# Layer seams of a fused two-block kernel: weights split ahead, and where the low part of the inputs is computed

## The chip, the cores and the metric

The kernel runs on one core of a Trainium2 chip. The metric is the time of one launch on the device in microseconds (us); the median over several runs counts. TensorE (PE) multiplies, VectorE (DVE), ScalarE (ACT) and GpSimd (POOL) do elementwise work, SyncE (SP) issues the loads. Each engine runs its own queue in order and waits for semaphores of the others.

## The reference, cut to what matters

Two blocks follow each other on a 512 x 1024 stream `x`, of two layers each. The first has an attention and convolution layer (called layer 0) and a gated recurrent one (layer 1), each closed by a scaled residual and a layer norm. The second block has an even mixer, an FFN, an odd mixer and an FFN:

```python
def rms_norm(x, g):
    y = x32 * rsqrt(mean(x32 * x32, axis=-1) + NORM_EPS) * g

def swiglu(x, w_gate, w_up, w_down):
    return (silu(x @ w_gate) * (x @ w_up)) @ w_down

for layer in range(DEPTH):
    hn = rms_norm(x, norm_mix_pre[layer])
    mix = even_mixer(hn, ...) if layer % 2 == 0 else odd_mixer(hn, ...)
    x = x + rms_norm(mix, norm_mix_post[layer])
    hn = rms_norm(x, norm_ffn_pre[layer])
    ff = swiglu(hn, w_gate[layer], w_up[layer], w_down[layer])
    x = x + rms_norm(ff, norm_ffn_post[layer])
```

The odd mixer is a projection, a convolution over four positions, two gates (matrix products), a linear recurrence and a product with a second, activated projection. Everything is float32.

## The kernel before

`x` lies transposed in SBUF: eight tiles `res_x` of 128 features x 512 positions. A matrix with float32 accuracy is multiplied in three passes: each operand is split into a rounded high part and a rest, and `product` (L303) runs high x high, high x low and low x high for each of the eight 128-blocks of the inner dimension, 24 matmuls for one output block.

`weights` (L244 and L250 through the helpers) loads a block of 128x1024 into `wp_r`, ACT copies it to the rounded `wp_h`, and DVE, or POOL where it is asked for, subtracts: `wp_l = wp_r - wp_h`. The pool has three `wp_r` and four of `wp_h` and `wp_l` each, so at most four split blocks are ahead.

The end of a layer is `out_products`: the first five output blocks over all columns, then the last three (`keep`) in two halves of 256 columns. `use` takes each result off PSUM (tiles `po_mx` in the mixers, `g_ff` in the FFN) and adds its square to `po_a`. `done(s)` then sums `po_a` over the features with a matmul against ones (the tile `z`), gets the reciprocal root (ACT, then the three DVE operations on `po_t` and `po_r`) and walks over the eight `m` of that half: a product with `po_r`, an update of `res_x`, and `pre(m, s)`. In layers 0 and 1 `deepnorm` has the same part with mean and variance (`n_a`, `n_m`, `n_r`).

`pre` (L1054) makes the next layer's inputs. ACT writes `pn_h = res_x * scale` (with a bias as well at the end of layer 1), ACT copies it to the rounded `act_h`, and POOL subtracts: `act_l = pn_h - act_h`. These are 16 tiles of 128x256 at each of four places: from layer 1 to the even mixer, from there to its FFN, from this FFN to the odd mixer, and from there to its FFN.

The next layer begins with `firsts`: three weight blocks, whose subtractions run on POOL, and the first three products, one half of the columns after the other, `k` by `k`, so that PE can start on a half as soon as its first `act_h` and `act_l` are there. The pre-norm's own scale (`res_acc`, summed by `rms` into the tile `g` or `z`) comes later and is multiplied onto the results, so the products don't wait for it. In the odd mixer `rms` stands right behind `firsts`; then come the convolution (`o_xb`, `o_xc`), whose split result `o_h` and `o_l` feeds the gates, products into `g`.

No order is written out by hand: a scheduler places each engine's instructions by priorities that follow the order of the program, and a tile of a pool is taken again when its last reader is done.

Of the kernel before, what the change touches and what calls it, by code (L numbers as in the profile page):

```python
# [188 lines left out]
class Prog:  # L189
    def __init__(self, es, tc, I, off):  # L190
        self.tc, self.nc, self.I, self.off, self.es = tc, tc.nc, I, off, es
        nc = self.nc
# [146 lines left out]
    def out_products(self, ps, block, xs, parts, use, done, keep=3, n=1024, late=(), begun=None, spare=(None, 0)):  # L339
# [108 lines left out]
    def layer0(self, stop=False):  # L448

        nc, tc = self.nc, self.tc  # L450
        with ExitStack() as es:
# [78 lines left out]
            self.out_products(ps, lambda m: self.I["wo_ab"][m], xs2, PARTS, use, done, spare=(Alloc(es, tc, "w0", {"h": (1, 1024), "l": (1, 1024)}), 1))  # L530
# [282 lines left out]
    def layer1(self):  # L813
        nc, tc = self.nc, self.tc
        with ExitStack() as es:
# [24 lines left out]
            self.out_products(ps, lambda m: self.I["wo_c"][m], xs2, PARTS[:2], use, done, spare=(Alloc(es, tc, "w5", {"h": (1, 1024), "l": (1, 1024)}), 1))  # L840
# [570 lines left out]
    def even(self):  # L1411
        tc = self.tc
        with ExitStack() as es:
# [6 lines left out]
            self.out_products(ps, lambda m: self.I["wo_ev"][m], xs2, PARTS[:2], use, done, late=(4, 5), begun=begun, spare=(Alloc(es, tc, "w6", {"h": (2, 1024), "l": (2, 1024)}), 2))  # L1420
# [213 lines left out]
    def odd(self):  # L1634
        tc = self.tc
        with ExitStack() as es:
# [235 lines left out]
```

## Time and profile before

| | |
|---|---|
| runs | 2127.01, 2133.92, 2132.29 us; median 2132.29 us |
| profiled execution | 2134.38 us, its span 2132.6 us |
| busy share of the span | PE 96%, DVE 63%, ACT 43%, POOL 20% |
| POOL on `act_l` | 64 operations, 56.6 us |
| POOL on `wp_l` | 27 operations, 69.4 us |

The shares are averages over a long program. In the middle of the layers PE is busy without a gap. The transitions are short stretches: layer 0 to layer 1 at 440 to 476 us, layer 1 to the even mixer at 898 to 968, even mixer to its FFN at 1173 to 1222, this FFN to the odd mixer at 1545 to 1612, odd mixer to its FFN at 1735 to 1784. A row's time in square brackets is how long the engine stood idle just before, and what released it. A row that ends in x4 is four instructions that ran on without a gap.

### The profile page before, as it was taken

To read this page: it belongs to the slowest core of one execution; us is meant where nothing else is said; L and a number is where in the kernel's file an instruction comes from. 1 tells how busy PE (TensorE), PEld (TensorE's weight loads), DVE (VectorE), ACT (ScalarE), POOL (GpSimd) and SP (SyncE) were. 2 spreads that over 40 slices of the span, in tenths; PEclk is the share of its full clock that TensorE was granted. 3 is DMA by queue.
4 is the path that set the end of the run, shared out by engine and by line. 5 is a ranking of instruction groups with operands and counts; after the bars stand their busy time and mean duration, and the time that the engine had idled before them with its cause. 6 is when DMAs were issued, how large, how long until landed. Compare 5 with 4: busy or idle time off the path is not lost.

```text
span 2132.6 us, 29872 instructions
## 1 busy us (share of the span) xinstructions
PE 2045.8 (96%) x11624; PEld 1740.2 (82%) x11624; DVE 1349.8 (63%) x2290; ACT 911.0 (43%) x1634; POOL 427.0 (20%) x403
## 2 busy tenths in 40 slices
PE   6999999999999999989999999999989799999997
PEld 4888888889888888888778888888877588888886
DVE  6775566786666665786665734535589886254455
ACT  2563343445433444455655533222356645322231
POOL 1111111354122221042112310101143322010011
PEclk9999999999999999999989999999999899999998
DMA  8344442321111111224423133333312232333231
GB/s 300 119 158 136 146 142 71 116 88 60 50 54 56 50 50 50 89 85 158 119 70 99 60 96 102 99 98 93 116 50 69 70 99 80 109 96 93 98 109 40
DMA packets 80142, 204.97 MB, mean 96 GB/s; under 512 B 19200, under 2 KB 28160, under 8 KB 80000
## 3 DMA queue, kind: packets, MB, share of 16 engines
q1 hardware_dynamic: 80000, 203.06, 30.1%
q8 instruction: 91, 1.49, 0.3%
q14 instruction: 51, 0.42, 0.1%
HBM read 188.87 MB, written 14.16 MB: 95 GB/s over the span
## 4 chain that ended last, share of the span: by engine, by line
PE 76%; DVE 13%; issue 5%; ACT 4%; POOL 1%; DMA 1%; SPq 0%; POOLq 0%; DVEq 0%; ACTq 0%
PE mm L313 56%; PE a L313 5%; PE mc L313 3%; PE x L313 2%; PE S L313 2%; DVE res_x L266 1%; PE s L313 1%; PE pt L651 1%; PE o L313 1%; DVE wp_l L250 1%; PE mc L425 1%; DVE o_xc L266 1%; DVE n_a L250 1%; ACT wp_h L244 1%; PE z L313 1%
## 5 line engine op out<-in xcount | busy, mean ns | idle before, releaser
L244 ACT ACTIVATE wp_h<-wp_r 128x1024 fp32r<-128x1024 f32 (+2 forms) x263 | 271.3, 1037 | 456.1 <-PE mm L313 263.4
L250 DVE TENSOR_TENSOR wp_l<-wp_r,wp_h 128x1024 fp32r<-128x1024 f32 (+1 forms) x236 | 326.9, 1388 | 108.7 <-ACT wp_h L244 108.6
L313 PE MATMUL mm<-act_h,wp_l 128*128 128x512 f32 (+1 forms) x1008 | 379.4, 376 | 12.0 <-DVE wp_l L250 10.2
L313 PE MATMUL mm<-act_l,wp_h 128*128 128x512 f32 (+1 forms) x1008 | 380.0, 377 | 1.9 <-POOL act_l L250 1.9
L313 PE MATMUL mm<-act_h,wp_h 128*128 128x512 f32 (+1 forms) x1008 | 379.8, 377 | 1.7 <-ACT wp_h L244 1.3
L313 PE MATMUL mm<-a_h,wp_h 128*128 128x512 f32 (+1 forms) x920 | 336.8, 367 | 5.5 <-ACT wp_h L244 3.3
L313 PE MATMUL mm<-a_h,wp_l 128*128 128x512 f32 (+1 forms) x920 | 329.8, 359 | 1.2 <-POOL wp_l L250 1.2
L313 PE MATMUL mm<-a_l,wp_h 128*128 128x512 f32 (+1 forms) x920 | 328.6, 358 | 0.9 <-DVE a_l L250 0.9
L313 PEld LDWEIGHTS mm<-act_h,wp_l 128*128 128x128 f32 x1008 | 194.0, 192 | 46.4 <-DVE wp_l L250 11.1
L313 PEld LDWEIGHTS mm<-act_l,wp_h 128*128 128x128 f32 x1008 | 193.6, 192 | 35.9 <-POOL act_l L250 2.6
L313 PEld LDWEIGHTS mm<-act_h,wp_h 128*128 128x128 f32 x1008 | 193.5, 192 | 34.7 <-ACT wp_h L244 1.8
L313 PEld LDWEIGHTS mm<-a_h,wp_h 128*128 128x128 f32 x920 | 174.1, 189 | 30.6 <-ACT wp_h L244 3.3
L313 PEld LDWEIGHTS mm<-a_l,wp_h 128*128 128x128 f32 x920 | 174.1, 189 | 25.9 <-issue 1.9
L313 PEld LDWEIGHTS mm<-a_h,wp_l 128*128 128x128 f32 x920 | 173.8, 189 | 24.6 <-POOL wp_l L250 1.4
L250 POOL TENSOR_TENSOR g_g<-g_g,g_u 128x512 f32<-128x512 f32 x44 | 61.1, 1390 | 549.3 <-DVE g_u L250 502.9
L313 PE MATMUL mm<-h_l,wp_h 128*128 128x512 f32 (+1 forms) x344 | 129.2, 376 | 0.6 <-DVE h_l L250 0.5
L313 PE MATMUL mm<-h_h,wp_h 128*128 128x512 f32 (+1 forms) x344 | 129.0, 375 | 0.3 <-ACT h_h L244 0.3
L313 PE MATMUL mm<-h_h,wp_l 128*128 128x512 f32 (+1 forms) x344 | 128.8, 374 | 0.0
L250 DVE TENSOR_TENSOR g_u<-mm,res_rr 128x512 f32<-128x512 f32 x44 | 30.4, 690 | 125.9 <-PE mm L313 125.9
L250 POOL TENSOR_TENSOR wp_l<-wp_r,wp_h 128x1024 fp32r<-128x1024 f32 x27 | 69.4, 2574 | 135.9 <-ACT wp_h L244 119.0
L244 ACT ACTIVATE m_km<-m_k 128x512 f32<-128x512 f32 x56 | 37.5, 672 | 122.9 <-DVE m_k L250 101.4
L247 ACT ACT_TABLE_LOAD x60 | 77.0, 1283 | 1.8 <-PEq L1860 0.7
(496 smaller groups left out, 3927.3 us busy)
## 6 DMA issues: line engine op xcount, KB each, us to landing
wp_r<-w_gu SPq DMA_DIRECT2D x88, 512.0 KB, 3.5
wp_r<-w_c SPq DMA_DIRECT2D x40, 512.0 KB, 3.5
wp_r<-wada SPq DMA_DIRECT2D x32, 512.0 KB, 3.7
wp_r<-w_d SPq DMA_DIRECT2D x32, 512.0 KB, 3.6
wp_r<-w_ab SPq DMA_DIRECT2D x26, 512.0 KB, 4.8
st_r<-wada SPq DMA_DIRECT2D x16, 512.0 KB, 7.9
wp_r<-w_od SPq DMA_DIRECT2D x16, 512.0 KB, 3.5
s_d<-s_s SPq DMA_DIRECT2D x24, 256.0 KB, 2.4
```

The source lines that it names most:

```text
L244: self.nc.scalar.activation(out=out, in_=in_, func=ACT.Copy, scale=scale)
L247: self.nc.scalar.activation(out=out, in_=in_, func=func, **kw)
L250: (eng or self.nc.vector).tensor_tensor(out=out, in0=a, in1=b, op=op)
L266: self.nc.vector.scalar_tensor_tensor(out=out, in0=a, scalar=s, in1=b, op0=op0, op1=op1)
L313: self.nc.tensor.matmul(out=out, lhsT=a, rhs=b, start=start, stop=stop)
L425: self.nc.tensor.matmul(out=p[32 * k:32 * k + 32, :], lhsT=self.sc[:, 4 * j + k, :], rhs=raw[j][:, k * 256:(k + 1) * 256], start=j == 0, s ...
L651: nc.tensor.transpose(pt[:, i * 128:(i + 1) * 128], P[h][:, i * 128:(i + 1) * 128], self.idn)
```

## The change

Two things change. First, `out_products` gets a list `after`, the next layer's first weight blocks; as many as buffers are free for (two after layers 0 and 1, three at the other places) are loaded and split, on DVE, ahead of the last products, and `firsts` takes them over and makes only the missing ones on POOL. Second, in `pre` without a bias ACT writes the rounded `act_h` directly from `res_x`, and one DVE operation gives `act_l = res_x * scale - act_h`; with a bias the three steps remain, with the subtraction on DVE. In the odd mixer the fourth product, `proj(3)`, is moved ahead of `rms`.

```diff
     def firsts(self, ps, blocks, xs, tags=("mm",) * 3):
-        ws = [self.weights(b, eng=self.nc.gpsimd) for b in blocks]
+        ws = self.ahead + [self.weights(b, eng=self.nc.gpsimd) for b in blocks[len(self.ahead):]]
+        self.ahead = []
...
-    def out_products(self, ..., begun=None, spare=(None, 0)):
+    def out_products(self, ..., begun=None, spare=(None, 0), after=()):
...
         ws = [self.weights(block(8 - keep + j), n, pool=pool if j < own else None) for j in range(keep)]
+        self.ahead = [self.weights(b) for b in after[:4 - keep + own]]
...
         def pre(k, s, x=None, scale=g, bias=None):
-            hi, lo = self.xs[k]
-            h = N("h")
+            hi, lo = (t[:, s] for t in self.xs[k])
             x = self.x[k][:, s] if x is None else x
             if bias is None:
-                self.act(h, x, ACT.Copy, scale=scale[:, k:k + 1])
+                self.act(hi, x, ACT.Copy, scale=scale[:, k:k + 1])
+                self.stt(lo, x, scale[:, k:k + 1], hi.bitcast(F32), ALU.mult, ALU.subtract)
             else:
+                h = N("h")
                 self.act(h, x, ACT.Identity, scale=scale[:, k:k + 1], bias=bias[:, k:k + 1])
-            self.copy(hi[:, s], h)
-            self.sub(lo[:, s], h, hi[:, s].bitcast(F32), nc.gpsimd)
+                self.copy(hi, h)
+                self.sub(lo, h, hi.bitcast(F32))
...
         first = dict(enumerate(self.firsts(ps, [self.I["w_od"][m] for m in range(3)], xs)))
+        first[3] = proj(3), None
         self.rms(ps("g"))
```

The five calls of `out_products` pass `after`: blocks of `w_c` after layer 0, `w_ev` (4, 8, 0) after layer 1, `w_gu0`, `w_od` and `w_gu1` after the others. The last FFN passes none.

On DVE, at the end of the first FFN, from the root of the first half (`po_r`) on, before (`g_ff` is the FFN's output, `mm` PSUM, `vecs` the scales):

```order
L250 TENSOR_TENSOR g_ff<-g_ff,mm 128x256
L250 TENSOR_TENSOR g_ff<-g_ff,po_r 128x256 x2
L250 TENSOR_TENSOR po_a<-po_a,po_sq 128x256
L266 SCALAR_TENSOR_TENSOR res_x<-g_ff,vecs,res_x 128x256 x2
L250 TENSOR_TENSOR g_ff<-g_ff,po_r 128x256 x2
L266 SCALAR_TENSOR_TENSOR res_x<-g_ff,vecs,res_x 128x256
L250 TENSOR_TENSOR g_ff<-g_ff,mm 128x256
L266 SCALAR_TENSOR_TENSOR res_x<-g_ff,vecs,res_x 128x256
L250 TENSOR_TENSOR g_ff<-g_ff,po_r 128x256
L250 TENSOR_TENSOR po_a<-po_a,po_sq 128x256
```

and now, from the same place on:

```order
L251 TENSOR_TENSOR g_ff<-g_ff,mm 128x256
L251 TENSOR_TENSOR g_ff<-g_ff,po_r 128x256 x2
L251 TENSOR_TENSOR po_a<-po_a,po_sq 128x256
L267 SCALAR_TENSOR_TENSOR res_x<-g_ff,vecs,res_x 128x256 x2
L251 TENSOR_TENSOR g_ff<-g_ff,po_r 128x256
L267 SCALAR_TENSOR_TENSOR act_l<-res_x,vecs,act_h 128x256 x2
L267 SCALAR_TENSOR_TENSOR res_x<-g_ff,vecs,res_x 128x256
L251 TENSOR_TENSOR g_ff<-g_ff,mm 128x256
L251 TENSOR_TENSOR g_ff<-g_ff,po_r 128x256
L267 SCALAR_TENSOR_TENSOR act_l<-res_x,vecs,act_h 128x256
L251 TENSOR_TENSOR po_a<-po_a,po_sq 128x256
L267 SCALAR_TENSOR_TENSOR res_x<-g_ff,vecs,res_x 128x256
```

The `act_l` operations have come into DVE's queue, between the updates and ahead of the additions to `po_a`; three of them stand ahead of this second `po_a`, and three more ahead of the last one.

On POOL, from the end of the even mixer to the start of the odd one, before (`g_g` is the FFN's gate product):

```order
L250 TENSOR_TENSOR wp_l<-wp_r,wp_h 128x1024 x3
L250 TENSOR_TENSOR act_l<-pn_h,act_h 128x256 x16
L250 TENSOR_TENSOR g_g<-g_g,g_u 128x512 x22
L250 TENSOR_TENSOR wp_l<-wp_r,wp_h 128x1024 x3
L250 TENSOR_TENSOR act_l<-pn_h,act_h 128x256 x4
L250 TENSOR_TENSOR wp_l<-wp_r,wp_h 128x1024
L250 TENSOR_TENSOR act_l<-pn_h,act_h 128x256 x9
L1675 MEMSET o_xb 128x3 x2
L250 TENSOR_TENSOR act_l<-pn_h,act_h 128x256 x3
L250 TENSOR_TENSOR wp_l<-wp_r,wp_h 128x1024 x2
```

and now:

```order
L251 TENSOR_TENSOR y_y<-y_y,e_vT 128x512 x4
L251 TENSOR_TENSOR g_g<-g_g,g_u 128x512 x22
L251 TENSOR_TENSOR wp_l<-wp_r,wp_h 128x1024
L1680 MEMSET o_xb 128x3 x2
L251 TENSOR_TENSOR wp_l<-wp_r,wp_h 128x1024 x2
```

What is left on POOL at these two transitions is the odd mixer's own weight subtractions and the FFN's products.

On PE, around `rms` of the odd mixer, before (the numbers tell the tiles apart: `mm_14664` is the fourth projection, `mm_14471` the third; `g_14616` is the sum of `rms`):

```order
L313 MATMUL mm_14471<-act_h_13928,wp_l_14466 128x256
L313 MATMUL mm_14664<-act_h_13914,wp_h_14660 128x512
L313 MATMUL mm_14664<-act_l_13915,wp_h_14660 128x512
L313 MATMUL mm_14664<-act_h_13914,wp_l_14661 128x512
L313 MATMUL mm_14664<-act_h_13916,wp_h_14660 128x512
L313 MATMUL g_14616<-res_acc_13931,ones1024_73 128x512
L313 MATMUL mm_14664<-act_l_13917,wp_h_14660 128x512
```

and now (`mm_14558` is the fourth projection, `mm_14683` the fifth):

```order
L315 MATMUL mm_14558<-act_h_13894,wp_l_14555 128x512
L315 MATMUL mm_14558<-act_h_13896,wp_h_14554 128x512
L315 MATMUL mm_14558<-act_l_13897,wp_h_14554 128x512
L315 MATMUL mm_14558<-act_h_13896,wp_l_14555 128x512
L315 MATMUL g_14583<-res_acc_13899,ones1024_73 128x512
L315 MATMUL mm_14683<-act_h_13882,wp_h_14679 128x512
```

Four of the 24 matmuls of the fourth projection stood ahead of the sum, and 45 of the fourth, fifth and sixth between it and the first gate; now all 24 stand ahead of it, and 16 of the fifth between it and the gates.

## Rows read from the trace of the kernel before

**Rows 1.** Windows view: us, busy us (instructions) of PE, PEld, DVE, ACT, POOL, clock, DMA.

```profile
898.00:968.00 70.00, 63.87 (x393) 58.60 (x392) 61.24 (x102) 37.04 (x69) 25.55 (x23) 0.95 0.31 98
1545.00:1612.00 67.00, 56.89 (x331) 49.71 (x330) 57.90 (x89) 36.65 (x69) 24.39 (x26) 0.92 0.15 48
```

**Rows 2.** PE's waits in 898:968, 1173:1222, 1545:1612, 1735:1784: total us, times, longest.

```profile
PE o L313 <- DVE res_x L266: 2.9, 1, 2.9
PE z L313 <- DVE n_a L250: 1.4, 1, 1.4
...
PE z L313 <- DVE po_a L250: 1.8, 1, 1.8
...
PE z L313 <- DVE po_a L250: 4.1, 1, 4.1
PE g L313 <- DVE res_acc L250: 3.9, 1, 3.9
PE g L313 <- DVE o_l L250: 1.7, 1, 1.7
...
PE z L313 <- DVE po_a L250: 2.7, 1, 2.7
```

**Rows 3.** Windows view of PE, odd mixer's end: us, busy (matmuls), granted clock, DMA.

```profile
1754.90:1758.30 3.40, 3.40 (x19) 0.50 0.00 0
1760.30:1763.70 3.40, 3.40 (x31) 1.00 0.00 0
```

**Rows 4.** Timeline of DVE, 1740 to 1772: start, length, line, out<-in, repeats.

```profile
1745.13 0.87 DVE L266 SCALAR_TENSOR_TENSOR res_x<-po_mx,vecs,res_x 128x256 f32<-128x256 f32 x2
1745.92 0.75 DVE L250 TENSOR_TENSOR po_mx<-po_mx,po_r 128x256 f32<-128x256 f32 x2
...
1748.77 0.96 DVE L250 TENSOR_TENSOR po_a<-po_a,po_sq 128x256 f32<-128x256 f32 x1
...
1751.92 0.81 DVE L266 SCALAR_TENSOR_TENSOR res_x<-po_mx,vecs,res_x 128x256 f32<-128x256 f32 x1
...
1753.00 0.94 DVE L250 TENSOR_TENSOR po_a<-po_a,po_sq 128x256 f32<-128x256 f32 x1
...
1755.87 0.42 DVE L266 SCALAR_TENSOR_TENSOR po_t<-z,po_r 128x256 f32<-128x256 f32 x1 [1.00 <-ACT po_r L247]
...
1761.33 1.84 DVE L266 SCALAR_TENSOR_TENSOR res_x<-po_mx,vecs,res_x 128x256 f32<-128x256 f32 x2
```

**Rows 5.** Timeline of POOL, the same stretch.

```profile
1746.94 3.39 POOL L250 TENSOR_TENSOR act_l<-pn_h,act_h 128x256 fp32r<-128x256 f32 x4 [12.98 <-ACT act_h L244]
...
1767.68 1.44 POOL L250 TENSOR_TENSOR act_l<-pn_h,act_h 128x256 fp32r<-128x256 f32 x2 [1.27 <-ACT act_h L244]
```

**Rows 6.** Timeline of DVE, 1545 to 1600.

```profile
1558.65 2.45 DVE L266 SCALAR_TENSOR_TENSOR res_x<-g_ff,vecs,res_x 128x256 f32<-128x256 f32 x1
...
1591.38 6.20 DVE L266 SCALAR_TENSOR_TENSOR o_xc<-o_xb,vecs,o_xc 128x512 f32<-128x512 f32 x6
```

**Rows 7.** Timeline of POOL, the same stretch.

```profile
1558.11 2.71 POOL L250 TENSOR_TENSOR wp_l<-wp_r,wp_h 128x1024 fp32r<-128x1024 f32 x1 [1.91 <-ACT wp_h L244]
```

**Rows 8.** Timeline of DVE, 905 to 960.

```profile
912.84 1.21 DVE L250 TENSOR_TENSOR wp_l<-wp_r,wp_h 128x1024 fp32r<-128x1024 f32 x1
...
931.82 3.45 DVE L250 TENSOR_TENSOR res_x<-res_x,n_r 128x256 f32<-128x256 f32 x2
...
938.46 0.96 DVE L250 TENSOR_TENSOR n_a<-n_a,n_sq 128x256 f32<-128x256 f32 x1
```

**Rows 9.** Timeline of PE, 1576 to 1602.

```profile
1584.25 2.08 PE L313 MATMUL g<-res_acc,ones 128*128 128x512 f32 x2 [3.90 <-DVE res_acc L250]
...
1597.63 1.21 PE L313 MATMUL g<-o_h,wp_h 128*128 128x512 f32 x4 [0.37 <-ACT o_h L244]
```

**Rows 10.** Timeline of POOL, 905 to 960.

```profile
955.95 1.45 POOL L250 TENSOR_TENSOR act_l<-pn_h,act_h 128x256 fp32r<-128x256 f32 x2
```

**Rows 11.** Timeline of ACT, 1740 to 1762.

```profile
1746.46 0.71 ACT L244 ACTIVATE act_h<-pn_h 128x256 fp32r<-128x256 f32 x2
```

More of the change, by code (lines that the diff above doesn't have):

```diff
@@ L299, in firsts @@
     def firsts(self, ps, blocks, xs, tags=("mm",) * 3):
-        ws = [self.weights(b, eng=self.nc.gpsimd) for b in blocks]
+        ws = self.ahead + [self.weights(b, eng=self.nc.gpsimd) for b in blocks[len(self.ahead):]]
+        self.ahead = []
         out = [ps(t) for t in tags]
@@ L337, in scores, with out_products @@
             self.matmul(out, q[h], k[:, cols], i == 0, i == 1)
-    def out_products(self, ps, block, xs, parts, use, done, keep=3, n=1024, late=(), begun=None, spare=(None, 0)):
+    def out_products(self, ps, block, xs, parts, use, done, keep=3, n=1024, late=(), begun=None, spare=(None, 0), after=()):
         wide = [X] + [s for s in parts if s.start >= L]
@@ L529, in layer0 @@
             use, done = self.deepnorm(N, ps, res, mod, emit)
-            self.out_products(ps, lambda m: self.I["wo_ab"][m], xs2, PARTS, use, done, spare=(Alloc(es, tc, "w0", {"h": (1, 1024), "l": (1, 1024)}), 1))
+            self.out_products(ps, lambda m: self.I["wo_ab"][m], xs2, PARTS, use, done, spare=(Alloc(es, tc, "w0", {"h": (1, 1024), "l": (1, 1024)}), 1), after=[self.I["w_c"][m] for m in range(3)])
     def layer0_mix(self, es, e0, late, xs, Y, first, s5):
@@ L839, in layer1 @@
             use, done = self.deepnorm(N, ps, self.x, self.mods[1], emit)
-            self.out_products(ps, lambda m: self.I["wo_c"][m], xs2, PARTS[:2], use, done, spare=(Alloc(es, tc, "w5", {"h": (1, 1024), "l": (1, 1024)}), 1))
+            self.out_products(ps, lambda m: self.I["wo_c"][m], xs2, PARTS[:2], use, done, spare=(Alloc(es, tc, "w5", {"h": (1, 1024), "l": (1, 1024)}), 1), after=[self.I["w_ev"][m] for m in (4, 8, 0)])
             for k in range(KT):
@@ L1419, in even @@
             use, done = self.postnorm(es, ps, "norm_mix_post", 0, pre)
-            self.out_products(ps, lambda m: self.I["wo_ev"][m], xs2, PARTS[:2], use, done, late=(4, 5), begun=begun, spare=(Alloc(es, tc, "w6", {"h": (2, 1024), "l": (2, 1024)}), 2))
+            self.out_products(ps, lambda m: self.I["wo_ev"][m], xs2, PARTS[:2], use, done, late=(4, 5), begun=begun, spare=(Alloc(es, tc, "w6", {"h": (2, 1024), "l": (2, 1024)}), 2), after=[self.I["w_gu0"][m] for m in range(3)])
             stats()
@@ L1642, in odd @@
             use, done = self.postnorm(es, ps, "norm_mix_post", 1, pre)
-            self.out_products(ps, lambda m: self.I["wo_od"][m], xs2, PARTS[:2], use, done, late=(2, 4), spare=(Alloc(es, tc, "w7", {"h": (3, 1024), "l": (3, 1024)}), 3))
+            self.out_products(ps, lambda m: self.I["wo_od"][m], xs2, PARTS[:2], use, done, late=(2, 4), spare=(Alloc(es, tc, "w7", {"h": (3, 1024), "l": (3, 1024)}), 3), after=[self.I["w_gu1"][m] for m in range(3)])
             stats()
@@ L1805, in ffn @@
                     use, done = self.postnorm(es, ps, "norm_ffn_post", l, pre, ff, last)
-                    self.out_products(ps, block, hs, PARTS[:2], use, done, n=n, keep=4 if last else 3, spare=(H, 2))
+                    self.out_products(ps, block, hs, PARTS[:2], use, done, n=n, keep=4 if last else 3, spare=(H, 2), after=() if last else [self.I["w_od"][m] for m in range(3)])
                     if stats:
```

## The prediction

> **What bounds the kernel now.** I read the windows view first, of the places that the change touches. They are the five where one layer ends and the next begins, called seams here: S1 layer 0 to layer 1, S2 layer 1 to even mixer, S3 even mixer to its FFN, S4 that FFN to odd mixer, S5 odd mixer to its FFN. In S2 PE works 63.9 of 70 us and VectorE (DVE) 61.2, in S4 56.9 and 57.9 of 67, GpSimd (POOL) about 25 in each [rows 1]. In the middle of the layers PE has few gaps that this change touches, so these must give what there is. PE's waits say what comes last in them: in S3, S4 and S5 the sum `z` waits for DVE's `po_a` (1.8, 4.1 and 2.7 us), in S4 the rms sum `g` waits 3.9 for DVE's `res_acc` and the gates 1.7 for `o_l`, and in S2 the waits are 2.9 and 1.4 [rows 2].
>
> A wait costs more than its length. The 3.4 us behind S5's wait have a granted clock of 0.50, which is 1.2 GHz, and 19 matmuls; 3.4 us at 1.00 (2.4 GHz) hold 31 [rows 3]. That is 1.3 us lost; I take 1.5 for each such piece, since some records may be missing, and 0.12 us for a matmul of 256 columns, twice that for 512.
>
> The third view is the timeline of DVE against that of POOL. In S5 two products of 128x256 on DVE take 0.75 and two updates of `res_x` 0.87; while POOL's four `act_l` run (1746.94 to 1750.33), an addition `po_a` among them takes 0.96, and two updates at 1761.33 take 1.84 [rows 4, 5]. In S4 one update takes 2.45 while a POOL `wp_l` runs [rows 6, 7]. So a DVE operation that reads two SBUF tensors appears to stand still until POOL's operation is over. This is the lever: what leaves POOL makes other DVE work shorter, while DVE must do the subtraction itself.
>
> The Trainium skill ("SBUF — State Buffer", section SBUF: two separate sides) says that GpSimd and a VectorE operation with two SBUF inputs exclude each other for a whole instruction; the rows agree. Another page of the Trainium skill speaks against the change: "Perfetto Trace Analysis", section Optimizing Scalar/DVE Operations, would offload a saturated DVE to ScalarE or even GpSimd, though it adds that the shared read port may undo the latter. By that rule the seams get slower, which is R3's case below.
>
> **The parts.** Counted on the built kernel: POOL loses 64 `act_l` and 13 `wp_l`, DVE gains these 77, ACT loses 48 scaled copies, PE's work is the same.
>
> Prices. Two updates start 0.79 before the operation behind them [rows 4], so one three-operand operation costs 0.40, and one product likewise 0.34. An `act_l` on DVE has no row; its nearest is the update, the same kind and shape: 0.40 free, 0.92 if slowed as at 1761.33 [rows 4]. I take 0.40, since with POOL's work gone nothing seen in the rows would slow it. Per seam that is 16 x 0.40 = 6.4 us more on DVE.
>
> *S5, worked in full.* Before, the last `po_a` ends at 1753.94 [rows 4] and the last `act_l` at 1767.68 + 1.44 = 1769.1 [rows 5]. In the new order six `act_l` stand ahead of the last `po_a` (+2.4). Against them: three slowed operations (one shown) return from 0.96 to 0.42 (-1.6), the last `po_a` itself from 0.94 (-0.5), an update from 0.81 to 0.40 (-0.4) [rows 4], and two products and an update now stand behind it (-1.1). Sum -1.2. PE has 30 matmuls of the next layer ahead of `z` where it had 19: 11 x 0.12 = 1.3 us of fill. 2.7 - 1.2 - 1.3 leaves a wait of 0.2, and with the wait the slow-clock piece (1.5) should go. What is late next is the second half of the columns. There DVE has a product, an update and an `act_l` per 128 rows, 1.14 us, against nine matmuls or 1.06 on PE, so DVE paces it. From the end of `po_a` (1752.7) to `po_t` it was 1.9 at the slow clock [rows 4], and I take 1.6; two `act_l` in between the three operations up to `po_r` make 2.1, and the rest is 8 x 1.14 plus one `res_acc` addition, 9.7. The last `act_l` ends at 1766.1, that is 3.0 earlier. Gain 3.0, between 1.2 (`po_a` alone) and 4.2 (wait and clock).
>
> *S3* is the same pattern. The wait is 1.8, `po_a` comes 0.8 earlier and 7 matmuls more of fill give 0.8, so it closes. But a `wp_l` (1.2 [rows 8]) that stood ahead of `po_a` now stands behind it, on the way to `po_t`, so the second half gains less: about 2.2. Gain 2.2, between 0.8 and 3.3.
>
> *S4.* `po_a` comes 2.5 earlier (three slowed operations, the 2.45 of [rows 6], two updates moved behind, less 2.4 for `act_l`), the fill is 12 matmuls more (1.4): 4.1 goes to 0.2. By the S5 reckoning the last `act_l` ends 4.5 earlier, the sum of squares `res_acc`, now hit by at most one POOL `wp_l`, gains 1.5 more, and `g` starts near 1578.2 instead of 1584.25 [rows 9], 6.0 earlier. PE doesn't wait there any more, since all 24 matmuls of the fourth product now stand ahead of `g` where 4 stood. But these are taken from the cover behind it: from `g` to the first gate product lie 13.4 us [rows 9], the way through `res_rr`, `o_xb`, the convolution `o_xc` (six updates in 6.2 [rows 6]) and `o_h`. Before, 45 matmuls filled this; now 16 do (3.8 us), and PE waits about 9 us for `o_h`, with a slow-clock piece behind (1.5). At the first gate PE has done 9 of these matmuls less than before (40 instead of 49; 9 x 0.24 = 2.2). So 6.0 - 2.2 - 1.5, and 1.7 back, as the next `o_l` now follows directly on DVE: 4.0. Behind it the mixer waits for DVE and ACT chains which then start 6.0 earlier; between 4.0 and 6.0 I take 4.5. Bounds: 0 (all given back at the gates) and 10 (all waits of S4).
>
> *S2.* Two of three POOL `wp_l` and all `act_l` leave. DVE's two products at 931.82 take 3.45 where two such take 0.75 (-2.7); the order up to the second `z`, relayed at free prices with its eight `act_l`, ends 3.2 before 939.4 [rows 8]. In the second half POOL alternates between `act_l` and scalings of `res_x`; relayed, it gains some 3 more, and the last `act_l`, which ended at 957.4 [rows 10], ends near 951. Two `wp_l` (2.4) come onto DVE ahead of the first `z`, where PE waited 1.4 already. The two waits of [rows 2] and two slow-clock pieces are 7.3 together, and more than that can't come back. I take 5, between 2 and 7.3.
>
> *S1 and the weights ahead.* In S1 two of the three first weights go to DVE early, but the third stays on POOL at its old place, and it is this one that PE's product waits for. Gain 0, between -1 and +1. Elsewhere the early split counts only as POOL time removed, which is in the sums above. The loads of these weights go through the same queue in nearly the same order: 0.
>
> The steady parts of FFNs and mixers are unchanged: 0. **Sum:** 3.0 + 2.2 + 4.5 + 5 = 14.7. The profiled execution took 2134.38 us (span 2132.6); it becomes 2119.7. The median of the runs is 2132.29, 2.1 lower: 2117.6, so 2118.
>
> **Rivals.**
> R1, *the waits only move.* `act_l` stands in DVE's queue and needs ACT's `act_h`, two of which take 0.71 [rows 11]; an update must end first, then ACT, then the handover, while DVE waits with all that is queued behind. At 0.3 for each of four to nine places per seam this is 1.2 to 2.7, in S2, S3 and S5 about 7 together, and S4 returns its 4.5 at the gates: 14.7 - 7 - 4.5 = 3.2 us, time 2129. For it: DVE is near full [rows 1]. Against it: the new order puts a product or an update between in most places.
>
> R2, *everything goes.* All these waits and the clock pieces vanish: 7.3 + 3.3 + 10 + 4.2 = 25, time 2107. For it: every one of the waits in S2, S3 and S5 hangs on a DVE operation that POOL slowed. Against it: the chain behind `g` in S4, and DVE's pace of 1.14 against 1.06.
>
> R3, *slower: DVE becomes the bound.* If DVE's long operations have another cause than POOL (traffic of ACT or PE, say), they stay long and the 16 `act_l` come on top. If half of these cost 0.92 and half 0.40, the second half's share is 5.3, less about 1.2 for the shorter way through ACT and POOL: 4 us later in each of S3, S4 and S5, nothing gained in S2: 2132 + 12 = 2144. It decides from the point at which a three-operand 128x256 operation there stays above 0.6. Against it: the long ones [rows 4, 6] lie inside POOL operations, and those outside are short.
>
> R4, *the change doesn't do what it says:* the weights were already split in time, so splitting ahead is worth nothing. My sum has that in it; only if `act_l` on POOL weren't the lever either, this gives 2132, and it shares R1's chance.
>
> **How the numbers follow.** Forecast, 2112 to 2124: 0.60. R1 with R4: 0.18. R2: 0.13. R3: 0.09. A measurement of this kernel can tell about 0.3% from no change, 6.4 us. The forecast and R2 lie wholly below 2125.9 (0.73), and with a sliver of R1: faster 0.74; same 0.18; slower 0.08. The range runs from 2106 (just below R2) to 2131 (R1 and half of R4), which leaves out R3 and a little of R4 and R2.
>
> **What would show it.** Right: in the changed trace no 128x256 DVE operation in S3 and S5 above 0.5; `act_l` near 0.40; the `z` waits of S3 to S5 below 0.5; `g` of S4 without a wait and a new wait of 7 to 10 us at the gates for `o_h`; POOL's busy time down by some 90 us (64 x 0.85 + 13 x 2.7 [rows 5, 7]). Wrong: DVE idle in the seams for ACT's `act_h` (R1), long DVE operations with POOL idle (R3), or a second half in S2 that waits for `act_l` as long as before.

## The result, and the profile after

The changed kernel took 2117.70 us in the median (2116.99 to 2120.27, four runs) beside 2131.19 us for the kernel before (2127.01 to 2133.92, four runs). The ratio is 0.9942, with a 95% interval of 0.9928 to 0.9956: 13.5 us less, about twice what such a measurement can tell from no change. The profiled execution took 2120.27 us with a span of 2118.5 us, so 14.1 us less between the spans.

The page of the changed kernel, its first part (busy us, share of the span, instructions):

```profile
PE 2041.6 (96%) x11624; PEld 1737.8 (82%) x11624; DVE 1340.2 (63%) x2367; ACT 896.2 (42%) x1586; POOL 337.4 (16%) x326
```

POOL went down from 427.0 to 337.4 us of work and DVE took over 77 operations, yet DVE's share of the span is 63% as before. So what DVE took over was paid for by what became shorter on it. DVE's own groups show where, in columns: operations | total us, mean ns of one | idle ahead. Before, the updates that stood beside POOL's work:

```profile
L266 DVE SCALAR_TENSOR_TENSOR res_x<-po_mx,vecs,res_x 128x256 f32<-128x256 f32 x32 | 20.9, 678 | 0.0
```

and after, the same updates and the new `act_l`:

```profile
L267 DVE SCALAR_TENSOR_TENSOR act_l<-res_x,vecs,act_h 128x256 fp32r<-128x256 f32 x48 | 21.3, 476 | 0.2 <-ACT act_h L248 0.2
L267 DVE SCALAR_TENSOR_TENSOR res_x<-po_mx,vecs,res_x 128x256 f32<-128x256 f32 x32 | 14.3, 476 | 0.0
```

An update fell from 678 to 476 ns in the mean, and `act_l` costs the same 476. The 48 `act_l` of S3 to S5 together waited 0.2 us for ACT's `act_h`; the 16 of S2, a group of their own, not at all.

In S5, the seam that the prediction worked in full, DVE's timeline now reads (start, us of the group, line, operation, how many); it answers to [rows 4]:

```profile
1736.59 0.88 DVE L267 SCALAR_TENSOR_TENSOR act_l<-res_x,vecs,act_h 128x256 fp32r<-128x256 f32 x2
1737.38 0.48 DVE L267 SCALAR_TENSOR_TENSOR res_x<-po_mx,vecs,res_x 128x256 f32<-128x256 f32 x1
...
1742.55 0.42 DVE L251 TENSOR_TENSOR po_a<-po_a,po_sq 128x256 f32<-128x256 f32 x1
...
1753.83 0.87 DVE L267 SCALAR_TENSOR_TENSOR res_x<-po_mx,vecs,res_x 128x256 f32<-128x256 f32 x2
...
1755.22 0.87 DVE L267 SCALAR_TENSOR_TENSOR act_l<-res_x,vecs,act_h 128x256 fp32r<-128x256 f32 x2
```

Nothing is stretched: the `po_a` addition takes 0.42 where it took 0.94 to 0.96, and two updates 0.87 where two took 1.84. PE no longer waits for `z` there.

PE's waits in S2, S3 and S4 (total us, times, longest) answer to [rows 2]; in S5 none is left:

```profile
PE mm L315 <- ACT act_h L245: 2.1, 1, 2.1
PE mm L315 <- DVE act_l L251: 1.2, 1, 1.2
PE o L315 <- DVE res_x L267: 0.2, 1, 0.2
...
PE mm L315 <- ACT act_h L248: 0.7, 1, 0.7
...
PE z L315 <- DVE po_a L251: 0.9, 1, 0.9
PE mm L315 <- DVE act_l L267: 0.8, 1, 0.8
```

Where the time went, from both traces: for every ACT, DVE and POOL operation that occurs equally often in the two, the difference of its starts; the median of these differences on each stretch of the program, and from stretch to stretch the step. A minus is time gained there against the kernel before, in us. The later rows are the experiments of the next section.

```
                    S1   S2    even   S3    S4 up to  odd    S5
                               mixer        the gates mixer
after              +1.4 -6.5   0.0  -3.2  -4.0      +2.8  -4.1
pre_only            0.0 -6.1  -1.5  -2.9  -4.7       0.0  -4.0
ahead_only         +1.5 -3.3   0.0   0.0  -0.1       0.0  -0.1
no_first3           0.0 -7.4  -3.6  -4.7  -4.7       0.0  -4.2
pool_idle_work      0.0 +1.1   0.0  +4.5  +2.9      +2.7  +3.7
pool_idle_memset   +1.6 -6.9  -1.2  -4.8  -4.6      +2.8  -4.1
sub_dve            +1.6 -7.4  -3.6  -4.4  -4.2      +2.8  -3.7
banks5             +1.2 -6.6  -1.6  -2.9  -4.8      -1.5  -4.1
nf3_banks5         +1.6 -6.6  -1.6  -2.9  -4.2      -3.7  -4.2
nf3_firsts_dve     -1.1 -8.5   0.0  -3.4  -4.7       0.0  -4.1
nf3_gate_pool      +1.5 -7.3  -3.6  -4.7  -1.9      +9.7  -4.1
nf3_odd_dve        -1.6 -6.6  -1.7  -3.0  -8.3      -6.6  -4.1
nf3_odd_dve2        0.0 -7.3  -3.6  -4.7  -8.9     -12.4  -4.9
```

The steps of the changed kernel add up to 13.6 of the 14.1 us. The table compares single profiled executions. The even mixer, whose code no kernel here changes, differs in it by up to 3.6 us, and its column ends inside a piece that runs at the low clock there. With the cut behind that piece (at 1120 us of the kernel before), no_first3 has -5.4 in the even mixer and -3.0 in S3, and sub_dve, nf3_gate_pool and nf3_odd_dve2 have nearly the same; pool_idle_memset has -3.9 and -2.9, and the changed kernel -0.3 and -2.9. So the -4.4 to -4.8 of the S3 column are about -3, as elsewhere, and steps of 1 to 5 us are read with this in mind (last section).

### The profile page after: what moved, and what is told of

It is laid out like the page before. It is cut to its first block, busy times and chain, and to the rows that moved or that the text cites. A ratio compares the mean times of both kernels' runs of the same rounds, so it can differ in the third digit from the quotient of the medians.

```text
span 2118.5 us, 29759 instructions
## 1 busy us (share of the span) xinstructions
PE 2041.6 (96%) x11624; PEld 1737.8 (82%) x11624; DVE 1340.2 (63%) x2367; ACT 896.2 (42%) x1586; POOL 337.4 (16%) x326
## 4 chain that ended last, share of the span: by engine, by line
PE 80%; DVE 11%; issue 4%; ACT 3%; DMA 1%; POOL 1%; SPq 0%; POOLq 0%; DVEq 0%; ACTq 0%
PE mm L315 60%; PE a L315 5%; PE mc L315 3%; PE x L315 2%; PE S L315 2%; PE s L315 1%; PE o L315 1%; PE pt L655 1%; PE mc L429 1%; DVE res_x L267 1%; DVE o_a L267 1%; DVE r_x L251 1%; DVE wp_l L251 1%; PE z L315 1%; PE pt L315 1%
## 5 line engine op out<-in xcount | busy, mean ns | idle before, releaser
L251 DVE TENSOR_TENSOR wp_l<-wp_r,wp_h 128x1024 fp32r<-128x1024 f32 (+1 forms) x249 | 341.9, 1374 | 113.1 <-ACT wp_h L245 113.0
L315 PE MATMUL mm<-a_h,wp_h 128*128 128x512 f32 (+1 forms) x920 | 337.4, 368 | 5.2 <-ACT wp_h L245 3.3
L315 PEld LDWEIGHTS mm<-h_l,wp_h 128*128 128x128 f32 x344 | 64.8, 188 | 13.5 <-DVE h_l L251 2.1
```

Of the source, the lines that this page charges most:

```text
L251: (eng or self.nc.vector).tensor_tensor(out=out, in0=a, in1=b, op=op)
L315: self.nc.tensor.matmul(out=out, lhsT=a, rhs=b, start=start, stop=stop)
```

## The experiments

The theory: the gain is that DVE no longer stands still beside POOL's reads (the new `pre`), and the weights split ahead add little. The rival: the early weights bring it. Behind that, one thing was not as forecast: the odd mixer gave back 2.8 us behind the gates.

### Which part brings the time

**pre_only** is the kernel before with the new `pre` alone.

```diff
-                self.act(h, x, ACT.Copy, scale=scale[:, k:k + 1])
+                self.act(hi, x, ACT.Copy, scale=scale[:, k:k + 1])
+                self.stt(lo, x, scale[:, k:k + 1], hi.bitcast(F32), ALU.mult, ALU.subtract)
...
-            self.sub(lo[:, s], h, hi[:, s].bitcast(F32), nc.gpsimd)
+                self.sub(lo, h, hi.bitcast(F32))
```

> The kernel before with the new pre alone (act_h in one ACT operation, act_l on DVE); weights split where they were, proj(3) behind rms. Theory (DVE stands still while POOL reads, so the gain is POOL's act_l gone from the ends of the layers): no DVE operation of 128x256 is stretched by an act_l any more, S3 and S5 gain nearly what the whole change gained there (3.2 and 4.1), S2 about half of its 6.5, since the POOL wp_l stay; time 2120 to 2124. Rival (the gain is the weights that are split ahead): S3 and S5 stay as before, time 2130 to 2132.

Measured: 2113.68 us, ratio 0.9919 (0.9904 to 0.9934). This part alone brings the whole gain, and 4 us more than the changed kernel, which has the moved `proj(3)` besides. The two parts without that line are no_first3 below, at 2112.08, so beside this part the weights ahead bring 1.6 us, less than the spread of the runs (2108.80 to 2114.57 here). The expected 2120 to 2124 was too high by more than 6: it had half of 6.5 for S2, and S2 gained 6.1.

**ahead_only** is the kernel before with `ahead` and the five `after` lists alone.

```diff
+        ws = self.ahead + [self.weights(b, eng=self.nc.gpsimd) for b in blocks[len(self.ahead):]]
+        self.ahead = []
...
+        self.ahead = [self.weights(b) for b in after[:4 - keep + own]]
```

> The kernel before with the weights split ahead alone; the old pre with act_l on POOL, proj(3) behind rms. Theory: only the stretches in which a POOL wp_l of 2.4 us held DVE gain: S2 2 to 3 us, S4 about 2, S3 below 1, S5 nothing, since no wp_l ran on POOL there; time 2125 to 2128. Rival (the gain is the weights): S2 and S4 gain as much as under the whole change, time near 2120.

Measured: 2128.81 us, ratio 0.9989 (0.9979 to 0.9998), some 2 us, and 0.8 above what was expected. By the table it gains in S2 alone (3.3), where weights that POOL split stood in the seam, and nothing in S3 to S5; in S4, where about 2 were expected, it is 0.1. The rival falls.

**no_first3** is the changed kernel with the fourth projection back behind `rms`.

```diff
         first = dict(enumerate(self.firsts(ps, [self.I["w_od"][m] for m in range(3)], xs)))
-        first[3] = proj(3), None
         self.rms(ps("g"))
```

> The changed kernel with proj(3) back behind rms in the odd mixer. Theory (the fourth product only moves PE's idle time from behind the sum g to ahead of it, since its result takes the last of four PSUM tiles and the fifth product then waits for o_xb): PE waits about 6 us ahead of g and nearly nothing behind it, time within 1.5 of the changed kernel, 2116 to 2120. Rival (the reordering carries the gain of S4): 3 to 4 slower, 2121.

Measured: 2112.08 us, ratio 0.9917 (0.99 to 0.9933). I had expected no difference to speak of, and 6 us of wait ahead of `g`, where 2.07 came; by the medians the moved line costs 5.6 us. The traces put 3.5 of that at its place: S4 and the odd mixer together give 1.2 in the changed kernel and 4.7 without the line. Most of what the two profiles differ by beyond that is a clock that fell for a shorter time in the even mixer of this one, so 3.5 is the figure that I trust.

### Whether POOL's reads are the lever

**pool_idle_work** leaves the changed kernel as it is and gives POOL one subtraction per `pre` again, into a scratch tile that nobody reads.

```diff
                 self.sub(lo, h, hi.bitcast(F32))
+            self.sub(N("d"), x, hi.bitcast(F32), nc.gpsimd)
```

> The changed kernel, and POOL in addition subtracts act_h from res_x into a scratch tile once per pre, at the places where act_l was; nothing reads the result. Theory (DVE stands still while POOL reads two SBUF tensors): DVE operations of 128x256 beside it go back to about 0.9, S3 and S5 lose most of their gain and the time rises by 6 to 12, to 2124 to 2130. Rival (the gain is the shorter way from res_x to act_l): nobody waits for POOL, the time stays within 1.5 of 2118.

**pool_idle_memset** keeps POOL busy for about as long, with three fills of 128x256 per `pre` that read nothing, behind a copy of one column on ACT so that they start at the same time.

```diff
+            d = N("d")
+            self.copy(d[:, 0:1], x[:, 0:1])
+            for i in range(3):
+                nc.gpsimd.memset(d, 0.0)
```

> The changed kernel, and POOL in addition writes zeros into a scratch tile, three operations of 128x256 per pre (0.31 us each in the trace of before), started by a small ACT copy at the places where act_l was; nothing reads the result. Counterpart of pool_idle_work, where POOL read two SBUF tensors. Theory (it is POOL's reading that holds DVE): POOL is as busy as there, the DVE operations of 128x256 beside it stay below 0.5, and the time is at most 5 above the changed kernel, 2117 to 2123, for the ACT copies. Rival (any POOL work holds DVE, or the trouble is POOL's semaphores): DVE operations are stretched to 0.7 or more, time above 2130.

Measured: 2145.85 us, ratio 1.0075 (1.006 to 1.009), with the subtractions, and 2116.07 us, ratio 0.9935 (0.9916 to 0.9954), with the fills. The first is 28 us slower than the changed kernel, and slower than the kernel before; the second is equal to the changed kernel. POOL's total work is alike in the two, as their pages' first parts say. With the subtractions:

```profile
PE 2050.1 (96%) x11624; PEld 1739.4 (81%) x11624; DVE 1370.3 (64%) x2367; ACT 896.6 (42%) x1586; POOL 397.0 (19%) x390
```

With the fills:

```profile
PE 2039.0 (96%) x11624; PEld 1734.3 (82%) x11624; DVE 1341.9 (63%) x2367; ACT 901.6 (43%) x1650; POOL 394.2 (19%) x518
```

The same two groups of DVE as above, first with the subtractions on POOL:

```profile
L267 DVE SCALAR_TENSOR_TENSOR act_l<-res_x,vecs,act_h 128x256 fp32r<-128x256 f32 x48 | 36.0, 782 | 0.2 <-ACT act_h L248 0.2
L267 DVE SCALAR_TENSOR_TENSOR res_x<-po_mx,vecs,res_x 128x256 f32<-128x256 f32 x32 | 19.0, 624 | 0.0
```

and then with the fills:

```profile
L267 DVE SCALAR_TENSOR_TENSOR act_l<-res_x,vecs,act_h 128x256 fp32r<-128x256 f32 x48 | 22.3, 479 | 0.0
L267 DVE SCALAR_TENSOR_TENSOR res_x<-po_mx,vecs,res_x 128x256 f32<-128x256 f32 x32 | 14.6, 478 | 0.0
```

One place shows it in the timeline. In S5 with the subtractions, DVE and POOL:

```profile
1755.77 1.88 DVE L267 SCALAR_TENSOR_TENSOR act_l<-res_x,vecs,act_h 128x256 fp32r<-128x256 f32 x2
...
1755.74 1.63 POOL L251 TENSOR_TENSOR pn_d<-res_x,act_h 128x256 f32<-128x256 f32 x2 [40.49 <-ACT act_h L248]
```

Two `act_l` that take 0.87 to 0.95 elsewhere take 1.88 while POOL's two subtractions run. In the same seam with the fills:

```profile
1740.88 0.95 DVE L267 SCALAR_TENSOR_TENSOR act_l<-res_x,vecs,act_h 128x256 fp32r<-128x256 f32 x2
...
1740.97 1.81 POOL L1072 MEMSET pn_d<- 128x256 f32 x6 [1.20 <-ACT pn_d L245]
```

Six fills that lie over the two `act_l` leave them as they are. So it is not that POOL works but that it reads SBUF. The Trainium skill ("SBUF — State Buffer", section SBUF: two separate sides) gives this as an exclusive lock between a GpSimd operation that reads SBUF and VectorE operations with two SBUF inputs; 782 against 479 ns agrees.

The trace of the kernel before shows more about which DVE operations are held. Here is one that reads PSUM (`mm`), while POOL's `act_l` run from 1552.82 on, and one that reads a single SBUF tensor besides two columns of scalars, while POOL splits a weight block from 1598.61 to 1601.02:

```profile
1552.87 0.41 DVE L250 TENSOR_TENSOR g_ff<-g_ff,mm 128x256 f32<-128x256 f32 x1
...
1598.70 2.61 DVE L263 TENSOR_SCALAR o_xc<-o_xb,vecs 128x512 f32<-128x512 f32 x1
```

The second is held as well, though it has one tensor: another like it takes 2.57 beside a split, and the six that lie beside no such work 0.54 to 0.55. The first is not held: eight operations that read `mm` lie nine tenths or more inside a POOL operation with two inputs there, and all have their usual time (0.42 for 128x256, 0.68 to 0.69 for 128x512).

My expectation for the subtractions, 2124 to 2130, was too low: I had reckoned that the old state would come back, but in this kernel DVE has its own `act_l` on top, and these stand still too, 0.3 us each in the mean.

**sub_dve** separates the saved step on ACT: `pre` keeps `pn_h` and the rounding copy, and only the subtraction moves from POOL to DVE.

```diff
-                self.act(hi, x, ACT.Copy, scale=scale[:, k:k + 1])
-                self.stt(lo, x, scale[:, k:k + 1], hi.bitcast(F32), ALU.mult, ALU.subtract)
+                self.act(h, x, ACT.Copy, scale=scale[:, k:k + 1])
...
+            self.copy(hi[:, s], h)
+            self.sub(lo[:, s], h, hi[:, s].bitcast(F32))
```

> The changed kernel, but pre keeps ACT's two steps (pn_h, then act_h) and DVE subtracts act_h from pn_h. Theory (the gain is POOL's reads gone): at most 4 us are lost, by two ACT operations of 0.3 to 0.5 in front of each act_l in DVE's queue, time 2117 to 2122. Rival (the gain is the one ACT step saved): most of the gain is lost, time 2126 or more.

Measured: 2117.00 us, ratio 0.9934 (0.9913 to 0.9954), the same as the changed kernel. The saved ACT copy is worth nothing that can be measured; leaving POOL is what counts.

### Why the odd mixer gives back

PE at the seam into the odd mixer after the change (start, us of the group; in brackets the idle time ahead and what ended it); it answers to [rows 9]:

```profile
1572.37 1.13 PE L315 MATMUL g<-res_acc,ones 128*128 128x512 f32 x2
...
1580.32 0.77 PE L315 MATMUL mm<-act_h,wp_h 128*128 128x512 f32 x1 [6.83 <-DVE o_xb L251]
...
1586.35 1.09 PE L315 MATMUL g<-o_h,wp_h 128*128 128x512 f32 x4
...
1637.70 0.79 PE L315 MATMUL mm<-act_h,wp_l 128*128 128x512 f32 x1 [3.58 <-POOL wp_l L251]
```

The sum `g` no longer waits, as forecast. But the fifth projection, which was to fill the time up to the gates, stands 6.83 us for `o_xb`, an operation that it doesn't read. `o_xb` is what empties the PSUM tile of an earlier projection: the odd mixer has four tiles `mm` (`psum(mm=4, g=4)`), and with the fourth projection moved ahead all four are full when the fifth wants one. The piece around the end of the wait runs at the low clock (0.50 is 1.2 GHz). The windows view (us, busy us of PE, PEld, DVE, ACT, POOL, granted clock, DMA):

```profile
1578.20:1585.00 6.80, 4.68 (x11) 3.74 (x12) 6.73 (x12) 0.00 (x0) 0.00 (x0) 0.52 0.27 96
```

In no_first3 the same three places read:

```profile
1563.91 1.13 PE L315 MATMUL g<-res_acc,ones 128*128 128x512 f32 x2 [2.07 <-DVE res_acc L251]
...
1569.06 0.58 PE L315 MATMUL mm<-act_h,wp_h 128*128 128x512 f32 x1 [1.94 <-DVE o_xb L251]
...
1624.77 0.50 PE L315 MATMUL mm<-act_h,wp_l 128*128 128x512 f32 x1 [1.82 <-POOL wp_l L251]
```

The waits are 2.07, 1.94 and 1.82 us in place of 0, 6.83 and 3.58.

**banks5** is the changed kernel with five `mm` tiles and three `g`.

```diff
-        ps = self.psum(mm=4, g=4)
+        ps = self.psum(mm=5, g=3)
```

> The changed kernel with five PSUM tiles for projections and three for gates in the odd mixer, instead of four and four. Theory (proj(3) ahead of the sum g takes the last of four tiles, so the fifth product has to wait for o_xb): the 6.8 us in which PE waits behind g for o_xb vanish, the fifth product runs there, its weights and the next ones come free earlier, and the time falls by 2 to 5 to 2113 to 2116. Rival (the tiles don't matter, PE waits for the chain through o_xb, o_xc and o_h anyway): the wait moves to the first gate product, time 2116 to 2119.

Measured: 2112.39 us, ratio 0.9908 (0.9888 to 0.9928), 5.3 us below the changed kernel. Its PE at the two places:

```profile
1577.13 0.47 PE L315 MATMUL mm<-act_h,wp_h 128*128 128x512 f32 x1 [1.35 <-DVE o_xb L251]
...
1583.88 0.95 PE L315 MATMUL g<-o_h,wp_h 128*128 128x512 f32 x3 [2.39 <-ACT o_h L245]
```

The wait of 6.83 became 1.35, and 2.39 at the gates for `o_h`, which is the wait that the prediction had named. The step in the odd mixer turned from +2.8 to -1.5. The gates start no sooner behind `g` (14.7 us in banks5, 14.0 in the changed kernel): what came back is that the fifth product and part of the sixth are done by then.

**nf3_banks5** has five tiles and the fourth projection at its old place.

```diff
-        first[3] = proj(3), None
...
-        ps = self.psum(mm=4, g=4)
+        ps = self.psum(mm=5, g=3)
```

> Five PSUM tiles for projections and three for gates, with proj(3) back behind rms. Theory (with enough tiles the place of proj(3) doesn't matter, with four it does): within 2 of the kernel with five tiles and proj(3) ahead, 2110 to 2114. Rival (proj(3) ahead of rms is a gain of its own once a tile is free): 3 to 5 slower than that, 2115 to 2118.

Measured: 2112.61 us, ratio 0.992 (0.9905 to 0.9935), the same as banks5. With five tiles the place of the fourth projection doesn't matter; with four it costs (2117.70 against 2112.08). And a fifth tile without the moved line brings nothing (2112.61 against 2112.08). So it was the tile that the moved line took, not the place.

### What else stands beside POOL's reads

All four kernels here start from no_first3.

**nf3_firsts_dve** lets DVE split the weights that are still missing in `firsts`.

```diff
-        ws = self.ahead + [self.weights(b, eng=self.nc.gpsimd) for b in blocks[len(self.ahead):]]
+        ws = self.ahead + [self.weights(b) for b in blocks[len(self.ahead):]]
```

> The changed kernel with proj(3) behind rms, and the missing first weights (the third block behind layers 0 and 1) split on DVE as well. Theory: PE's wait of 1.2 for POOL's wp_l behind layer 0 falls below 0.5, and the third block behind layer 1 no longer holds DVE for 2.4; time 2109 to 2112. Rival (DVE is full there, its queue delays the split or the n_a sums): 0 to 3 lost, 2112 to 2115.

Measured: 2112.03 us, ratio 0.9912 (0.9891 to 0.9934), no change against no_first3: only two blocks are concerned, one each in S1 and S2. In its trace PE's wait for POOL's `wp_l` behind layer 0 is gone (1.1 in no_first3) and S1 and S2 come 1.1 earlier each; but its even mixer has the long piece at the low clock, and whether the edit is worth anything is open.

**nf3_gate_pool** attacks the longest wait of the odd mixer, 9.97 us for a `wp_l` that DVE splits late. In the changed kernel it is this row of PE, and below it the same wait in the kernel before (total us, times, longest, from 1612 to 1712):

```profile
1678.97 0.80 PE L315 MATMUL mm<-act_h,wp_l 128*128 128x512 f32 x1 [9.97 <-DVE wp_l L251]
...
PE mm L313 <- DVE wp_l L250: 10.2, 2, 10.0
```

All waits there sum to 16.8 us, so what stands ahead of the prediction, that PE is busy without a gap in the middle of the layers, does not hold for this one. The edit gives the late split to POOL, which was idle more.

```diff
-                px = proj(8 + 2 * b + i, nc.vector)
+                px = proj(8 + 2 * b + i)
```

> The changed kernel with proj(3) behind rms, and the weights of the odd mixer's second projections split on POOL instead of DVE. Theory (POOL's reads hold DVE, so what is off DVE's queue is paid there by stretched operations, but the split no longer stands behind the scan): the 10 us in which PE waits for wp_l near the mixer's end fall to 4 to 7, time 2106 to 2111. Rival (each POOL wp_l of 2.4 holds DVE's chain for as long): nothing gained or 2 to 5 lost, 2112 to 2117.

Measured: 2126.76 us, ratio 0.9978 (0.9966 to 0.999), 15 us worse than no_first3 and worse than either expectation. Its POOL, and PE's waits from 1590 to 1710 us:

```profile
1667.85 8.37 POOL L251 TENSOR_TENSOR wp_l<-wp_r,wp_h 128x1024 fp32r<-128x1024 f32 x3
...
PE mm L315 <- ACT wp_h L245: 10.9, 3, 6.6
PE mm L315 <- POOL wp_l L251: 8.8, 3, 3.6
```

The one long wait of 9.97 is gone, but six others sum to 19.7: all waits are 20.8 us here where no_first3 has 15.6 from 1590 to 1690. S4, too, gains only 1.9 where no_first3 gains 4.7. POOL takes 2.8 us for one block. That this holds DVE up meanwhile fits what is shown above, but over half of the 19.7 ends with ACT's `wp_h`, and why ACT came late was not traced further.

**nf3_odd_dve** goes the other way: the weight splits of the odd mixer's projections and gates on DVE (three of its output product stay on POOL).

```diff
-            w = self.weights(self.I["w_od"][m], eng=eng or nc.gpsimd)
+            w = self.weights(self.I["w_od"][m], eng=eng)
...
-            w = self.weights(self.I["w_rg"][b], eng=nc.gpsimd)
+            w = self.weights(self.I["w_rg"][b])
```

> The changed kernel with proj(3) behind rms, and all weights of the odd mixer split on DVE, none on POOL. Theory (a POOL wp_l of 2.4 holds DVE about as long as DVE needs for the split and more, 1.8 against 1.2): DVE gets no busier in effect, the waits for POOL wp_l vanish, time 2106 to 2111. Rival (in DVE's queue the splits stand behind the scan's chain, as the one does for which PE waits 10 us): PE waits longer, time 2114 to 2122.

Measured: 2102.89 us, ratio 0.9874 (0.9857 to 0.9891), 9 us below no_first3. At the end of the first FFN, DVE in the changed kernel, and POOL beside it:

```profile
1547.37 3.02 DVE L267 SCALAR_TENSOR_TENSOR res_x<-g_ff,vecs,res_x 128x256 f32<-128x256 f32 x2
...
1567.22 5.10 DVE L251 TENSOR_TENSOR res_acc<-res_acc,pn_sq 128x512 f32<-128x512 f32 x4
...
1547.69 2.41 POOL L251 TENSOR_TENSOR wp_l<-wp_r,wp_h 128x1024 fp32r<-128x1024 f32 x1 [44.44 <-ACT wp_h L245]
...
1568.12 2.84 POOL L251 TENSOR_TENSOR wp_l<-wp_r,wp_h 128x1024 fp32r<-128x1024 f32 x1 [17.95 <-ACT wp_h L245]
```

and the first place in nf3_odd_dve, where DVE does the split itself:

```profile
1546.38 0.87 DVE L267 SCALAR_TENSOR_TENSOR res_x<-g_ff,vecs,res_x 128x256 f32<-128x256 f32 x2
1547.17 1.21 DVE L251 TENSOR_TENSOR wp_l<-wp_r,wp_h 128x1024 fp32r<-128x1024 f32 x1
```

Two updates and the split take 2.08 on DVE together, less than the 3.02 of the two updates alone beside POOL's split. On DVE the split costs 1.21; on POOL it cost DVE 3.02 - 0.87 = 2.15. S4's step goes from -4.7 in no_first3 to -8.3. The rival had PE wait longer for splits in DVE's queue; the wait of 9.97 fell to 3.43 instead, so it falls.

**nf3_odd_dve2** adds the recurrence's products of 128x512, the last large POOL work in the odd mixer but for the three splits of the output product.

```diff
-                self.mul(r0, r0, i0, nc.gpsimd)
+                self.mul(r0, r0, i0)
```

> The kernel with proj(3) behind rms and all of the odd mixer's weights split on DVE, and in addition the eight products o_tr of 128x512 of the recurrence on DVE instead of POOL, so that POOL reads nothing there. Theory (each POOL o_tr of 1.7 holds DVE's chain o_mu, o_a, o_tr, scan for longer than DVE needs for the product, 0.6): the chain gets shorter by 1 to 2 per block of four, time 2096 to 2101. Rival (DVE is full in the mixer, and POOL's products ran beside ACT's part of the chain): the same or up to 4 slower, 2102 to 2107.

Measured: 2094.86 us, ratio 0.9837 (0.9819 to 0.9854), the fastest kernel of this study: 35 us below the kernel before (its median beside these runs was 2130.25) and 23 below the changed one. In nf3_odd_dve a DVE operation beside such a product on POOL (two of them from 1648.19 to 1651.69) reads:

```profile
1648.87 1.67 DVE L267 SCALAR_TENSOR_TENSOR o_a<-o_mu,o_a 128x512 f32<-128x512 f32 x1
```

and now the product on DVE, and the same operation behind it:

```profile
1643.01 0.68 DVE L251 TENSOR_TENSOR o_tr<-o_tr,o_ti 128x512 f32<-128x512 f32 x1
1643.61 0.68 DVE L267 SCALAR_TENSOR_TENSOR o_a<-o_mu,o_a 128x512 f32<-128x512 f32 x1
```

The operation falls from 1.67 to 0.68, and the product costs 0.68. The Trainium skill ("Perfetto Trace Analysis", section Optimizing Scalar/DVE Operations) suggests GpSimd for what saturates VectorE, with the reserve that the shared port may undo it; in the odd mixer here the reserve decides, +15 us one way and, against no_first3, -9 with the splits and -17 with the products as well the other.

## Why the prediction was right, point by point

The forecast was 2118, and 2117.70 came. The direction and the mechanism held; the places did not each hold, and the sum is so near because errors of both signs met.

**The lever held.** The prediction asked that no 128x256 DVE operation in S3 and S5 take over 0.5; none does (480 ns at most). Two `act_l` at 1736.59 start 0.79 before the operation behind them, so 0.40 each, as the prediction reckoned; 476 ns is one alone, from its start to its end. POOL lost 89.6 us where some 90 were named. The `z` waits went to 0, 0.91 and 0 in S3, S4 and S5, and the 0.91 is above the 0.5 that was named. R3, DVE as the bound, had its test at 0.6 per three-operand operation and falls, since only one of S4 beside a POOL `wp_l` is above it; pool_idle_work shows that it does come when POOL reads beside these operations (782 ns, and 15 us slower than the kernel before).

**S5: 3.0 forecast, 4.1 came.** The last `po_a` ends 1.5 earlier where 1.2 was worked out: 1742.97 against 1753.94, less the 9.5 us by which the seam is entered earlier. The last `act_l` ends at 1756.1, 3.5 earlier where 3.0 was worked out. The slow-clock piece went too. It lies inside the bound of 4.2.

**S3: 2.2 forecast, 3.2 came** (2.9 with the cut behind the low clock); the wait for `z` closed, and 0.7 for `act_h` is what is late next. It lies at the upper bound of 3.3.

**S2: 5 forecast, 6.5 came.** Of the two waits of [rows 2] 0.2 is left, and 2.1 and 1.2 at the first products stand in their place. S2 gains 3.3 in ahead_only, 6.1 in pre_only and 6.5 to 7.4 with both, so the two parts pay in part for the same waits and don't add.

**S1: 0 forecast, +1.4 came,** a clock matter. The same code there, from the windows view of PE alone (us, busy us, clock, DMA), after:

```profile
472.40:475.80 3.40, 3.40 (x14) 0.51 0.21 72
```

and before:

```profile
472.60:476.00 3.40, 3.40 (x27) 1.00 0.12 41
```

PE is busy throughout in both, with 14 matmuls against 27. pre_only and no_first3 don't have this step and ahead_only does, but no_first3 has the same weights ahead as the changed kernel, so I put it down to no part of the change. What sets it is open.

**S4: 4.5 forecast; 4.0 came up to the gates, and 2.8 of them were given back in the odd mixer, so 1.2.** This is the step that failed, at two points.

First, "`po_a` comes 2.5 earlier": its end came 0.6 earlier. DVE's row before, and after:

```profile
1561.02 0.94 DVE L250 TENSOR_TENSOR po_a<-po_a,po_sq 128x256 f32<-128x256 f32 x1
...
1552.50 0.41 DVE L251 TENSOR_TENSOR po_a<-po_a,po_sq 128x256 f32<-128x256 f32 x1
```

The ends lie 9.0 apart, of which 8.4 came in with the stretch, as the first `z` of the seam shows (1547.16 and 1538.75). The sum took the 2.45 of [rows 6] as gone with the POOL `wp_l` of [rows 7]. That `wp_l` did not leave. It is the fourth block's, which is not among the three split ahead; it stands on POOL at the same place, also in the order on POOL that is printed with the change, and the two updates beside it take 3.02 where two take 0.87. The last `act_l` then ended 2.4 earlier where 4.5 was worked out. A second POOL `wp_l`, which the prediction had allowed for, stretches four `res_acc` additions to 5.10. Hence `g` started 3.5 earlier, not 6.0 (1572.37 against 1584.25 is 11.9, of which 8.4 came in with the stretch).

Second, "16 now fill this": the prediction counted the matmuls in PE's queue between `g` and the gates as cover, and put the wait of about 9 us at the gates for `o_h`. The wait came, as 6.83 us, but ahead of the fill and for `o_xb`, since the fill needed a PSUM tile that was not empty. banks5 shows the cause by removing it. So the price of the moved projection was a tile and not the order: 3.5 us by the traces, 5.3 to 5.6 by the medians.

**The weights ahead: 0 forecast by themselves.** ahead_only gives some 2 us, so this was right in size; R4 falls nevertheless, since `act_l` was the lever. R1, that DVE waits for ACT's `act_h`, falls with 0.2 us over 64 operations. R2's 2107, everything gone, is not reached by the two parts without the moved line either (2112); but nf3_odd_dve2 goes beyond it with the same lever, in the middle of the odd mixer, where the prediction had looked for nothing.

## What to carry to other kernels

Before work is left on GpSimd because it is idle, price what it holds up: compare a VectorE operation that reads SBUF beside it and away from it (two updates took 1.84 against 0.87 us here), and move the work to VectorE if the hold costs more than doing it there (2.15 against 1.21 us for a weight block at the place shown). And when a product is moved ahead in the order, count the PSUM tiles of its pool as one counts engines: the wait shows on the next product, as a wait for an operation that it doesn't read.

## What was not expected of the hardware

How long the clock stays low differs between the profiles in code that is the same in all kernels. In the even mixer PE runs from the same place on at a granted clock of 0.50 (1.2 GHz). Before and after (windows of PE alone), first before:

```profile
1096.20:1116.70 20.50, 19.74 (x87) 0.50 0.08 26
```

after:

```profile
1090.00:1110.50 20.50, 19.43 (x85) 0.51 0.09 26
```

and no_first3, where the clock came back earlier:

```profile
1088.00:1094.80 6.80, 6.80 (x35) 0.50 0.24 80
...
1096.00:1108.00 12.00, 11.09 (x88) 1.00 0.01 2
```

It is 20.5 us at 1.2 GHz in the one and 6.8 in the other, and 5.4 us of time between no_first3 and the kernel before; in pre_only, banks5, nf3_banks5 and nf3_odd_dve it is 17.1 us. What sets the length is open: the runs don't tell whether it is the distance from the seam ahead or chance. The four executions of no_first3 alone spread from 2108.13 us, the profiled one, at a mean granted clock of 0.991, to 2116.31 us at 0.985, so it may well differ between executions of one kernel. It means that 2 to 5 us between two kernels, single profiles above all, can come from code that neither of them touches.
